# Differential attention in a token mixer: scores of each map from its own 32 channels instead of from masked copies of the keys

## The chip, the cores and the metric

The kernel runs on one core of a Trainium2 chip. The metric is the device time of one execution in microseconds; of several runs the median is given. Engines are named as in the profile: PE is TensorE's matmul, PEld its weight load, DVE VectorE, ACT ScalarE, POOL GpSimd, SP SyncE, which issues the DMAs.

## What is computed

Two networks run one after the other on a sequence of 256 tokens with 1024 features, batch 1, in float32. The first is one block (gated linear attentions, a recurrent unit, a convolved feed-forward part). The second has two layers of: feed-forward, token mixers, feed-forward, each with a layer norm. The token mixers are four attentions side by side (window, MLA, axial, differential) whose outputs are joined and multiplied by `w_out`. The change lies in the differential one, four heads, each with two maps of 32 channels (`DIFF_HEADS = 4`, `DIFF_QK = 32`, `DIFF_V = 64`):

```python
def _mixer_diff(d, lam_params, subln_g, slopes, layer_idx):
    q, k, v = jnp.split(d, [H * 2 * DIFF_QK, H * 4 * DIFF_QK], axis=-1)
    q = q.reshape(B, S, H, 2, DIFF_QK)
    k = k.reshape(B, S, H, 2, DIFF_QK)
    ...
        s = jnp.einsum('bqhmd,bkhmd->bhmqk', qi, k).astype(jnp.float32) * scale + bias[None, :, None]
        p = jax.nn.softmax(s, axis=-1)
        w = p[:, :, 0] - lam * p[:, :, 1]
        return jnp.einsum('bhqk,bkhd->bqhd', w.astype(v.dtype), v)
    ...
    o = _rms_norm(o, subln_g) * (1.0 - lam_init)
```

So each head has two score matrices, each over 32 channels of its own, two softmaxes, and the difference of the two.

## The kernel before

All 256 tokens stay on the chip, in two tiles of 128. Weights stream in from memory in pieces; each is split into a high and a low part (`piece`, line 92: ACT writes the high part, DVE or POOL the rest), and every product of activations and weights is three matmuls (`mm3`, lines 131 to 133; in the feed-forward parts lines 208 to 214 and 346). Attention scores and the products with the values are plain float32 matmuls.

`mixers2` (line 481) is the token mixer and runs once for each of the two layers. Its order is a plan written out by hand (line 732), which `weave` (line 449) plays: tokens such as `d2`, `u1` or `m0` are projections, `ax0`, `win0`, `mla0`, `diff0` queue the units of an attention for a token tile, and each `-` starts the next unit and takes each unit that is under way one stage further, the newest first. A unit is one head pair or, for `diff`, one head. After the plan comes the output projection (`contract`, line 745, its matmuls in lines 208, 211 and 214), in chunks that become ready as the attentions finish. This is the order of the program; within the data's dependencies a scheduler reorders each engine's instructions ahead of the launch, by a simulated timeline, and places the buffers and the semaphores.

The differential attention before the change:

- `diff_in` (line 639) is called as `d2` for the keys and as `d0` for the queries. The projection gives channels by tokens: 128 rows are 4 (head, map) pairs of 32 channels, two such groups `j`. For the keys, `d2` writes four copies of the projection into `dk` (line 637), copy `r` being multiplied by a column of 0 and 1 (`dmask`) that keeps the 32 channels of pair `r` alone. For the queries, `d0` writes one scaled copy, `dq`. `evac` (line 472) does each copy, alternately on ACT (line 475) and on DVE (lines 477, 479). `dk` shares its buffer (`tag="kzd"`) with `ct6`, a tile that the projection `u1` (`mla_up`) reads last.
- `diff(t)` (line 677) makes four units for token tile `t`. A unit for head `2 j + i` computes both maps with one matmul: all 128 rows of `dq`, times copies `2 i` and `2 i + 1` of `dk`, 512 columns (line 683). The zeros in the copies leave the right 32 channels.
- `softmax_head` (line 363) adds the bias and takes the maximum on DVE, one instruction for each map (line 379), then ACT takes the exponential (line 383). The unit goes on with the difference of the maps (lines 687 to 690), transposes on PE (line 149) and, in the last unit of a tile, the product with the values (line 704).
- The scores of all units, the outputs of the products with the values (lines 430, 434, 704) and some projections take their PSUM buffers from one pool, `mm`, of four, one bank each.

Other lines that are spoken of: 658 computes the scores of the window and axial attentions, from 64 rows (0 to 63 for unit 0, 64 to 127 for unit 1), two matmuls of 256 columns per unit into one buffer; 672 those of MLA, 96 rows; 928, in the first network, is a small matmul over 16 rows; 430 and 434 multiply by values with 64 columns of weights; 712 and 126 are DVE instructions that read the outputs of such products.

Of the kernel before, what the change touches and what calls it, by code (L numbers as in the profile page):

```python
# [11 lines left out]
F32 = mybir.dt.float32  # L12
F32R = mybir.dt.float32r
# [6 lines left out]
P = 128  # L20
T = 256
# [48 lines left out]
class Net:  # L70
# [292 lines left out]
    def softmax_head(self, ps, bias):  # L363


        nc, small = self.nc, self.small
        p = self.mix.tile([P, 2, T], F32, name="p_t", bufs=5)
        nm = small.tile([P, 2], F32, name="nm")
        sums = small.tile([P, 2], F32, name="sums")
        sink = None  # L370
        if bias is None:
            src = ps
            nc.vector.tensor_reduce(nm, ps, AX.X, ALU.max, negate=True)
        else:
            src = p
            mx = small.tile([P, 2], F32, name="mx")
            for j in range(2):
                tab, slope, sink = bias[j]
                nc.vector.tensor_tensor_reduce(p[:, j, :], ps[:, j, :], tab, -slope, -3e38 if sink is None else sink,
                                               ALU.add, ALU.max, mx[:, j : j + 1])  # L380
            nc.vector.tensor_scalar(nm, mx, -1.0, None, ALU.mult)
        for j in range(2):
            nc.scalar.activation(p[:, j, :], src[:, j, :], AF.Exp, bias=nm[:, j : j + 1], accum_out=sums[:, j : j + 1])
        es = None
        if sink is not None:
            es = small.tile([P, 2], F32, name="es")
            for j in range(2):
                nc.scalar.activation(es[:, j : j + 1], bias[j][2], AF.Exp, bias=nm[:, j : j + 1])
        return p, sums, es
# [91 lines left out]
    def mixers2(self, mix, l, post):  # L481
        nc, io = self.nc, self.io
        self.mix = mix
        pp, C = self.pp, self.C
        tsls = [slice(t * P, (t + 1) * P) for t in range(NT)]
# [5 lines left out]
        sink, gq, gk, lam4 = bp[:, 0:4], bp[:, 4:68], bp[:, 68:132], bp[:, 132:260]  # L491
# [33 lines left out]
            return groups[nm]  # L525

        kro = [mix.tile([P, 32], F32, name=f"kro{t}") for t in range(NT)]
        ct6 = mix.tile([P, 6, T], F32R, name="ct6", tag="kzd")
        cth, ctl = ct6[:, 0:3, :], ct6[:, 3:6, :]
        axv = mix.tile([P, NT, P], F32, name="axv")  # L530
        axq = mix.tile([P, 2, T], F32, name="axq")
# [102 lines left out]


        dq = mix.tile([P, 2, T], F32, name="dq")
        dk = mix.tile([P, 2, 4, T], F32, name="dk", tag="kzd")

        def diff_in(js):
            ks, n = group("diff")  # L640
            ps = self.proj_bank([P, 2, T])
            for j in js:
                self.proj_feat(ks, ps[:, j % 2, :], lambda w: w[:, j * P : (j + 1) * P])
                if j < 2:
                    self.evac(dq[:, j, :], ps[:, j, :], C["difq"][:, j : j + 1])
            if js[0] == 2:
                for r in range(4):
                    self.evac(dk[:, :, r, :], ps, C["dmask"][:, r : r + 1])


        slopes = [2.0 ** -(i + 1) for i in range(8)]
# [25 lines left out]
        def diff(t):  # L677
            hold = {}

            def run(j, i):  # L680
                h = 2 * j + i
                ps = self.mm.tile([P, 2, T], F32, name="mm_t")
                nc.tensor.matmul(ps, lhsT=dq[:, j, tsls[t]], rhs=dk[:, j, 2 * i : 2 * i + 2, :], start=True, stop=True)  # L683
                yield
                p, sums, _ = self.softmax_head(ps, [(C["dist"][:, t * T : (t + 1) * T], slopes[4 + h], None)] * 2)
                yield
# [585 lines left out]
    def setup(self):  # L1272
# [8 lines left out]
        for nm, w in CONSTS:  # L1281
# [5 lines left out]
        return ctile  # L1287


CONSTS = (("dist", 512), ("distw", 512), ("mlc", 64), ("mls", 64), ("axc", 128), ("axs", 128), ("winq", 2), ("difq", 2),  # L1290
          ("dmask", 4))
NCONST = sum(w for _, w in CONSTS)


def constants():

    f = np.float32
    pos = np.arange(T)
    dist = np.abs(pos[:, None] - pos[None, :]).astype(f)
    distw = np.where(dist <= 128, dist, f(1e32)).astype(f)  # L1300

    def angles(p, dim):
        inv = (f(10000.0) ** (-np.arange(0, dim, 2, dtype=f) / f(dim))).astype(f)
        a = p.astype(f)[:, None] * inv[None, :]
        return np.cos(a).astype(f), np.sin(a).astype(f)

    def tok(a):
        return a.reshape(NT, P, -1).transpose(1, 0, 2).reshape(P, -1)

    c, s = angles(pos, 32)  # L1310
    out = {"dist": tok(dist), "distw": tok(distw), "mlc": tok(np.concatenate([c, c], 1)),
           "mls": tok(np.concatenate([-s, s], 1))}
    cr, sr = angles(pos // 64, 32)
    cc, sc = angles(pos % 64, 32)
    out["axc"] = tok(np.concatenate([cr, cr, cc, cc], 1))
    out["axs"] = tok(np.concatenate([-sr, sr, -sc, sc], 1))
    p = np.arange(P)
    winq = np.zeros((P, 2))
    difq = np.zeros((P, 2))
    for j in range(2):  # L1320
        head = 2 * (p // 64) + j
        winq[:, j] = -0.125 * 2.0 ** (head + 1)
        head = 2 * j + p // 64
        difq[:, j] = -(32.0 ** -0.5) * 2.0 ** (head + 5)
    out["dmask"] = (p[:, None] // 32 == np.arange(4)).astype(f)
    out["winq"], out["difq"] = winq.astype(f), difq.astype(f)
    return np.ascontiguousarray(np.concatenate([out[nm] for nm, _ in CONSTS], 1).astype(f))

# [126 lines left out]
```

## Time and profile before

| | |
|---|---|
| median of 3 runs | 1340.91 us (1339.16 to 1342.98) |
| the profiled execution's own time | 1341.36 us |
| its span, first to last instruction | 1339.6 us |
| mean granted TensorE clock in the span | 0.994 |
| busy: PE, PEld | 1299.8 us (97%), 1092.4 us (82%) |
| busy: DVE, ACT, POOL | 887.1 us (66%), 730.3 us (55%), 558.8 us (42%) |
| chain of waits: PE, POOL, DVE, issue | 80%, 7%, 5%, 3% |

The span begins with the first instruction and ends with the last, so the execution's own time is somewhat longer. Matmuls are pipelined: the duration of a record reaches beyond the start of the next, and the distance between the starts tells what one costs. A granted clock of 1.00 is TensorE's full 2.4 GHz, 0.50 is 1.2 GHz. The token mixers lie between 525 and 645 us (first layer) and between 1022 and 1143 us (second layer). A float32 matmul shows as two records and an fp32r one as one.

### The profile page before, as it was taken

The numbers are of one execution on the slowest core, as the hardware profiler recorded it, in microseconds if no ns is written. First come the engines' busy times: TensorE is split into PE (matmuls) and PEld (weight loads), VectorE is DVE, ScalarE is ACT, GpSimd is POOL, SyncE is SP. The second block draws the span as 40 slices with busy tenths as digits, with TensorE's granted clock in tenths as the row PEclk, the third lists the DMA queues.
The fourth block names the chain that finished last, engine by engine and source line by source line (L and its number), as shares of the span: only waits on it lengthen the run. The fifth ranks groups of instructions, "written<-read, shape, count | busy, mean of one in ns | idle before, by whom it ended". The sixth has DMA issues, their size and how long they took to land.

```text
span 1339.6 us, 19335 instructions
## 1 busy us (share of the span) xinstructions
PE 1299.8 (97%) x7028; PEld 1092.4 (82%) x7028; DVE 887.1 (66%) x1402; ACT 730.3 (55%) x1282; POOL 558.8 (42%) x542
## 2 busy tenths in 40 slices
PE   7888899999999999999999999999999999999997
PEld 6767788888888888877888888888888877888886
DVE  5798588863667736677767645576726678766644
ACT  5775466654555543475556644465533666565540
POOL 5563433333533335830534434343436831434430
PEclk9999999999999999999999999999999999999999
DMA  6523545575655564550565564655664550655560
GB/s 220 189 64 118 188 157 186 186 217 166 216 172 187 186 213 147 181 168 7 187 211 185 185 220 146 217 189 189 209 191 138 165 159 1 219 190 188 188 205 32
DMA packets 63922, 227.19 MB, mean 170 GB/s; under 512 B 7105, under 2 KB 8145, under 8 KB 63058
## 3 DMA queue, kind: packets, MB, share of 16 engines
q1 hardware_dynamic: 63826, 225.95, 52.5%
q8 instruction: 55, 0.90, 0.3%
q14 instruction: 41, 0.34, 0.1%
HBM read 224.88 MB, written 1.05 MB: 169 GB/s over the span
## 4 chain that ended last, share of the span: by engine, by line
PE 80%; POOL 7%; DVE 5%; issue 3%; DMA 2%; ACT 2%; SPq 0%; DVEq 0%; ACTq 0%; POOLq 0%
PE mm_t L346 38%; PE acc_t L214 5%; PE acc_t L208 5%; PE acc_t L211 5%; PE mm_t L208 3%; PE mm_t L214 3%; PE mm_t L211 3%; POOL wl_t L111 3%; PE mm_t L133 3%; PE mm_t L131 3%; PE mm_t L132 3%; PE tp_t L149 2%; PE mm_t L430 1%; PE mm_t L683 1%; PE acc_t L131 1%
## 5 line engine op out<-in xcount | busy, mean ns | idle before, releaser
L111 POOL TENSOR_TENSOR wl_t<-raw,wh_t 128x512 fp32r<-128x512 f32 (+3 forms) x270 | 407.6, 1532 | 580.1 <-ACT wh_t L108 558.8
L111 DVE TENSOR_TENSOR wl_t<-raw,wh_t 128x1024 fp32r<-128x1024 f32 (+2 forms) x272 | 393.0, 1451 | 246.2 <-ACT wh_t L108 245.2
L108 ACT ACTIVATE wh_t<-raw 128x1024 fp32r<-128x1024 f32 (+2 forms) x407 | 416.5, 1039 | 232.3 <-PE mm_t L214 134.2
L346 PE MATMUL mm_t<-xx,wh_t 128*128 128x512 f32 x1456 | 501.6, 398 | 0.0
L346 PE MATMUL mm_t<-xx,wl_t 128*128 128x256 f32 x1456 | 379.4, 281 | 0.0
L346 PEld LDWEIGHTS mm_t<-xx,wh_t 128*128 128x128 f32 x1456 | 261.7, 188 | 49.3
L346 PEld LDWEIGHTS mm_t<-xx,wl_t 128*128 128x128 f32 x1456 | 274.9, 189 | 16.8
L349 DVE TENSOR_TENSOR sum<-sum,mm_t 128x256 f32<-128x256 f32 x182 | 74.4, 413 | 34.5 <-ACT sum L348 34.5
L348 ACT ACTIVATE sum<-mm_t 128x256 f32<-128x256 f32 x182 | 67.7, 372 | 39.0 <-PE mm_t L346 39.0
L208 PE MATMUL mm_t<-wh_t,hh 128*128 128x512 f32 x218 | 85.2, 391 | 0.0
L131 PE MATMUL mm_t<-wh_t,xx 128*128 128x512 f32 (+2 forms) x224 | 84.3, 376 | 0.8 <-ACT xx L125 0.8
L208 PE MATMUL acc_t<-wh_t,hh 128*128 128x512 f32 x218 | 84.9, 389 | 0.0
L211 PE MATMUL mm_t<-wl_t,hh 128*128 128x512 f32 x218 | 84.8, 389 | 0.0
L211 PE MATMUL acc_t<-wl_t,hh 128*128 128x512 f32 x218 | 84.8, 389 | 0.0
L132 PE MATMUL mm_t<-wl_t,xx 128*128 128x512 f32 (+2 forms) x224 | 83.5, 373 | 0.0
L133 PE MATMUL mm_t<-wh_t,xx 128*128 128x512 f32 (+2 forms) x224 | 82.6, 374 | 0.1
L214 PE MATMUL acc_t<-wh_t,hl 128*128 128x512 f32 x218 | 71.8, 389 | 0.0
L125 ACT ACTIVATE hh<-ht 128x256 fp32r<-128x256 f32 x72 | 30.1, 418 | 71.5 <-DVE ht L294 71.5
L214 PE MATMUL mm_t<-wh_t,hl 128*128 128x512 f32 x218 | 68.1, 389 | 0.0
L131 PE MATMUL acc_t<-xx,wh_t 128*128 128x256 f32 x176 | 52.3, 297 | 4.9 <-ACT wh_t L108 2.7
L126 DVE TENSOR_TENSOR hl<-ht,hh 128x256 fp32r<-128x256 f32 x72 | 37.8, 525 | 25.8 <-ACT hh L125 25.6
L292 ACT ACTIVATE sum<-sum 128x256 f32<-128x256 f32 x72 | 29.5, 409 | 41.7 <-DVE sum L349 41.7
(336 smaller groups left out, 2066.2 us busy)
## 6 DMA issues: line engine op xcount, KB each, us to landing
raw<-in_wgu_dram SPq DMA_DIRECT2D x176, 512.0 KB, 4.4
raw<-in_wd_dram SPq DMA_DIRECT2D x109, 512.0 KB, 4.4
raw<-in_gv_dram SPq DMA_DIRECT2D x42, 512.0 KB, 4.5
raw<-in_w_in_dram SPq DMA_DIRECT2D x36, 512.0 KB, 4.4
raw<-in_wo_dram SPq DMA_DIRECT2D x24, 512.0 KB, 3.7
gb<-in_ln_dram SPq DMA_DIRECT2D x6, 1024.0 KB, 4.7
raw<-in_w_in_dram SPq DMA_DIRECT2D x16, 384.0 KB, 3.5
raw<-in_w_in_dram SPq DMA_DIRECT2D x8, 416.0 KB, 3.5
```

What stands on the lines that cost most here:

```text
L108: nc.scalar.activation(hv, raw, AF.Copy)
L111: eng.tensor_tensor(lv[:, x : x + m], raw[:, x : x + m], hv.bitcast(F32)[:, x : x + m], ALU.subtract)
L126: self.nc.vector.tensor_tensor(dst_l, src, dst_h.bitcast(F32), ALU.subtract)
L131: mm(out, lhsT=lhs[0], rhs=rhs[0], start=start, stop=False, **kw)
L132: mm(out, lhsT=lhs[0], rhs=rhs[1], start=False, stop=False, **kw)
L133: mm(out, lhsT=lhs[1], rhs=rhs[0], start=False, stop=stop, **kw)
L208: m = self.nc.tensor.matmul(ps[t][h], lhsT=lh, rhs=wh[:, sl], start=first, stop=False)
L211: self.nc.tensor.matmul(ps[t][h], lhsT=lh, rhs=wl[:, sl], start=False, stop=False)
L214: self.nc.tensor.matmul(ps[t][h], lhsT=ll, rhs=wh[:, sl], start=False, stop=last)
L346: nc.tensor.matmul(out, lhsT=lhsT, rhs=rhs, start=k == 0 and i == 0, stop=k == NK - 1 and i == 1)
L348: nc.scalar.activation(r, ps[:, 1, :], AF.Copy)
L349: nc.vector.tensor_tensor(r, r, ps[:, 0, :], ALU.add)
```

## The change

The keys are kept once, as the projection gives them, without masks (`dk` has a quarter of its size), and `dk` and `ct6` get buffers of their own. A unit issues two matmuls, one for each map, over the 32 rows `64 i + 32 m` onwards of `dq` and `dk`, 256 columns each, into two buffers of the pool `mm`; `softmax_head` takes the list of the two. The constants lose the four columns of `dmask`.

```diff
@@ softmax_head
-                nc.vector.tensor_tensor_reduce(p[:, j, :], ps[:, j, :], tab, -slope, -3e38 if sink is None else sink,
+                nc.vector.tensor_tensor_reduce(p[:, j, :], ps[j] if isinstance(ps, list) else ps[:, j, :], tab, -slope, -3e38 if sink is None else sink,
                                                ALU.add, ALU.max, mx[:, j : j + 1])
@@ mixers2
-        ct6 = mix.tile([P, 6, T], F32R, name="ct6", tag="kzd")
+        ct6 = mix.tile([P, 6, T], F32R, name="ct6")
...
-        dk = mix.tile([P, 2, 4, T], F32, name="dk", tag="kzd")
+        dk = mix.tile([P, 2, T], F32, name="dk")
@@ diff_in
             if js[0] == 2:
-                for r in range(4):
-                    self.evac(dk[:, :, r, :], ps, C["dmask"][:, r : r + 1])
+                self.evac(dk, ps)
@@ diff, run
                 h = 2 * j + i
-                ps = self.mm.tile([P, 2, T], F32, name="mm_t")
-                nc.tensor.matmul(ps, lhsT=dq[:, j, tsls[t]], rhs=dk[:, j, 2 * i : 2 * i + 2, :], start=True, stop=True)
+
+                ps = [self.mm.tile([P, T], F32, name="mm_t") for _ in range(2)]
+                for m in range(2):
+                    a = slice(64 * i + 32 * m, 64 * i + 32 * m + 32)
+                    nc.tensor.matmul(ps[m], lhsT=dq[a, j, tsls[t]], rhs=dk[a, j, :], start=True, stop=True)
                 yield
@@ constants
-CONSTS = (("dist", 512), ("distw", 512), ("mlc", 64), ("mls", 64), ("axc", 128), ("axs", 128), ("winq", 2), ("difq", 2),
-          ("dmask", 4))
+CONSTS = (("dist", 512), ("distw", 512), ("mlc", 64), ("mls", 64), ("axc", 128), ("axs", 128), ("winq", 2), ("difq", 2))
...
-    out["dmask"] = (p[:, None] // 32 == np.arange(4)).astype(f)
```

## Rows read from the trace of the kernel before

**Rows 1.** View by windows: stretch, its us, busy us (instructions) of PE, PEld, DVE, ACT, POOL, PEclk, DMA.

```profile
595.00:645.00 50.00, 49.75 (x269) 34.97 (x268) 40.34 (x137) 30.50 (x88) 10.70 (x9) 1.00 0.17 54
645.00:860.00 215.00, 214.50 (x1096) 181.77 (x1095) 133.75 (x171) 111.75 (x168) 88.57 (x62) 1.00 0.61 198
...
1092.00:1143.00 51.00, 51.00 (x268) 35.10 (x267) 42.31 (x138) 30.45 (x87) 11.61 (x8) 1.00 0.17 53
```

**Rows 2.** Timeline of PE, around a diff unit: start us, us, engine, line, operation.

```profile
1108.69 1.02 PE L683 MATMUL mm_t<-dk,dq 128*128 128x512 f32 x2
1109.56 0.60 PE L149 MATMUL tp_t<-ident,p_t 128*128 128x128 f32 x4
```

**Rows 3.** Timeline of PE, around two MLA score units.

```profile
587.83 1.89 PE L672 MATMUL mm_t<-mqk 96*128 96x256 f32 x8
589.56 0.60 PE L149 MATMUL tp_t<-ident,p_t 128*128 128x128 f32 x4
```

**Rows 4.** Line 658: ns min/median/max, first and last start; 567.0 to 568.2, 573.4 to 574.6.

```profile
L658 PE MATMUL mm_t<-axk,axq x8: 376/376/480, 567.1 to 567.8; 64*128 64x256 f32 x8
...
L658 PE MATMUL mm_t<-wk,wq x4: 376/376/480, 573.5 to 574.3; 64*128 64x256 f32 x4
```

**Rows 5.** Timeline of PE, around the 16-row matmul of the first network.

```profile
46.99 0.69 PE L928 MATMUL mm_t<-glr,gup 16*128 16x256 f32 x2
47.62 0.39 PE L132 MATMUL acc_t<-xx,wh_t 128*128 128x256 f32 x1
```

**Rows 6.** Timeline of PE, around one 64-row unit among full-height matmuls.

```profile
573.00 0.60 PE L149 MATMUL tp_t<-ident,p_t 128*128 128x128 f32 x4
573.53 1.13 PE L658 MATMUL mm_t<-wk,wq 64*128 64x256 f32 x4
574.59 0.50 PE L131 MATMUL acc_t<-wh_t,ct 128*128 128x512 f32 x1
574.93 0.40 PE L132 MATMUL acc_t<-wl_t,ct 128*128 128x512 f32 x1
575.16 0.39 PE L133 MATMUL acc_t<-wh_t,ct 128*128 128x512 f32 x1
```

**Rows 7.** Timeline of PE, the first two diff units of the first layer.

```profile
594.56 1.08 PE L430 MATMUL mm_t<-pts,wdv 128*64 128x256 f32 x4
595.57 1.13 PE L683 MATMUL mm_t<-dk,dq 128*128 128x512 f32 x2
596.53 0.60 PE L149 MATMUL tp_t<-ident,p_t 128*128 128x128 f32 x4
596.97 1.02 PE L683 MATMUL mm_t<-dk,dq 128*128 128x512 f32 x2
```

**Rows 8.** Timeline, two diff units back to back; DVE's reads of two other buffers.

```profile
615.74 1.98 PE L683 MATMUL mm_t<-dk,dq 128*128 128x512 f32 x4
...
617.65 1.08 PE L430 MATMUL mm_t<-pts,axv 128*64 128x256 f32 x4
...
618.53 0.42 DVE L712 TENSOR_TENSOR do<-mm_t,ms 128x256 f32<-128x256 f32 x1
...
619.19 0.42 DVE L126 TENSOR_TENSOR ol<-mm_t,oh 128x256 fp32r<-128x256 f32 x1 [0.24 <-ACT oh L125]
```

**Rows 9.** Tile dk, its evacuations: ns min/median/max, first and last start.

```profile
L479 DVE TENSOR_SCALAR dk<-acc_t,ctile x4: 737/744/750, 584.2 to 1083.7; 128x512 f32<-128x512 f32 x4
L475 ACT ACTIVATE dk<-acc_t,ctile x4: 680/688/690, 585.8 to 1082.9; 128x512 f32<-128x512 f32 x4
```

**Rows 10.** Chain that ended last: first diff score and last projection matmuls, both layers.

```profile
595.63 1.06 PE mm_t L683 x2
...
641.12 0.66 PE acc_t L214 x2
...
1092.78 1.06 PE mm_t L683 x2
...
1139.47 0.66 PE acc_t L214 x2
```

## The prediction

> **What bounds the kernel now.** I read the stages first (the view by windows), then TensorE's instructions in order of time, then single lines and the chain of waits. The change touches only the token mixers of the second network, which run twice. The second half of each, where all the attention units run, is full of matmuls: PE is busy 49.75 of 50 us in one layer and 51.00 of 51 in the other, at a granted clock of 1.00 (the 2.4 GHz level), with DVE at about four fifths and ACT at three fifths; the stage behind has PE busy 214.5 of 215 us [rows 1]. A busy PE says little by itself, but the starts of the matmuls follow each other at their normal distance, because the scheduler fills every gap with matmuls of the output projection (lines 208 to 214). So in this half a microsecond of matmul time saved is a microsecond saved, as long as such fillers are ready, and a microsecond wasted is paid.
>
> **The score matmul now.** Each float32 matmul shows as two records. A diff unit (line 683) has two records of 512 columns over the full 128 rows: from its start to the next instruction 0.87 us, or 0.43 a record [rows 2]. There are 16 units: 2 layers, 2 token tiles, 4 heads. A record of 256 columns takes half of that: eight of line 672 last 1.73 us, 0.216 each [rows 3].
>
> **The score matmul afterwards: two maps, 32 rows each, 256 columns, two records each.** No row shows 32 channels in two maps at once; the nearest are the 64-row scores of line 658. There, eight records (two units, on rows 0 to 63 and 64 to 127, a buffer each) start between 567.1 and 567.8, while four records of one unit alone start between 573.5 and 574.3 [rows 4]: eight cost the time of four. So matmuls on different rows of the array run side by side, and a pair of maps should cost the time of one: 2 x 0.216 = 0.43 us instead of 0.86. The 16-row matmul of line 928 shows that a quarter-height one has the same pace: 0.63 us for two records [rows 5], as against 2 x 0.216 plus the 0.20 that comes next.
>
> That 0.20 is the price of changing the array's form. Around the lone four records: four transposes take 0.53 us up to the start where four take 0.44 elsewhere [rows 6, 7], so 0.09 to enter; the four records last 1.06, not 0.86, so 0.20 for a weight load that nothing covers and for leaving; and the first full-height matmul behind lasts 0.34 where the next lasts 0.23, so 0.11 [rows 6]. In all 0.40 us for a visit among full-height work. Half-width matmuls (lines 430, 434, 64 columns of weights) are a form of their own as well: a diff unit right behind one lasts 0.96, not 0.86 [rows 7], and four records between two of them last 1.91, not 1.72 [rows 8]. Some of the price is therefore paid already.
>
> The 16 units by what stands around them in the trace:
> - Five lie between full-height matmuls, as one does in [rows 2]. Now 0.86; then 0.09 + 0.20 + 0.43 + 0.01 (the second map's offset) + 0.11 = 0.84. Saved 0.02 each, 0.1 in all.
> - Four follow a half-width matmul and precede full-height work [rows 7]. Now 0.96; then 0.20 + 0.43 + 0.01 + 0.11 = 0.75. Saved 0.21 each, 0.84.
> - One lies between a half-width matmul and a 64-row one. Now 0.96 + 0.09; then 0.64. Saved 0.41.
> - Three times two units stand back to back behind a half-width matmul, as in [rows 8]: six units. If the two are parted by full-height work, the savings are 0.23 once and 0.43 twice, 1.1 in all. If they stay together but run one after the other, 2.3. If all four maps run abreast, 3.6.
>
> I take 1.1 for the last, because of the buffers. The score pool has four, and a unit now takes two of them. At 615.74 two others are still held: one is read by DVE at 618.53, one at 619.19 [rows 8]. The first unit then takes the remaining two, and the second must wait until DVE has read the first. Read in the same way, four of the 16 units start with fewer than two buffers free. Sum: 0.1 + 0.84 + 0.41 + 1.1 = 2.45, say **2.5 us less**; the bounds of the pair's cost are 5.0 less (3.6 for the last term) and, if the maps of a pair don't overlap at all, 16 x 0.43 = 6.9 more than the forecast, so 4.4 more than now.
>
> The Trainium skill (TensorE: Matmul & The Clock Gate, Part 3, "The mechanism") says that matmuls start and end strictly in program order. By that rule a pair would be three records deep, not two, since the second map's first pass stands behind the first map's second, and the sum would be 1341.9. The trace doesn't bear the rule out: in the program all four records of one unit of line 658 stand ahead of the other's, and yet they share the time [rows 4].
>
> **The other edits.** dk is one evacuation per layer instead of four of 0.69 to 0.74 us, two on each engine [rows 9]. That frees at least 2.1 us of ACT and DVE per layer, but the evacuations start at 584.2 to 585.8 in the first layer and the first score that reads dk starts at 595.57 [rows 7, 9]. I cost it at nothing: some 7 us of cover. Were the cover gone, three evacuations in series would be 2.1 us a layer, 4.2 in all. dk also leaves the buffer that it shared with ct6; the matmuls that read ct6 (u1) are issued on PE ahead of the projection that feeds dk, so this wait ends nothing. The constants lose 4 of 1416 columns, on one DMA far ahead of use; nothing else moves on SP or POOL. The softmax's two DVE reads go to two buffers; same instructions.
>
> Line 473 alternates the engines at every evacuation. With one where four were, all later evacuations up to the next dk change engine. The two layers run the same program with opposite alternation now and show what this and other chance of the schedule are worth: from the first diff score to the last projection matmuls of the chain 45.5 us in one, 46.7 in the other [rows 10], so up to 1.2 us a layer, either way. I take zero and put 2.4 into the range.
>
> The profiled execution took 1341.36 us, its span 1339.6; it stands 0.45 above the median of 1340.91. Against its own time the sum gives 1338.9, against the median **1338.4**.
>
> **Rivals.** A measurement of this kernel can tell about 0.3%, 4.0 us, from no change.
> - *More than the forecast.* The back-to-back units go abreast, or the schedule gains by the freed ACT and DVE time. For it: the eight records in the time of four [rows 4], and DVE at four fifths. Against it: the held buffers. 5.0 less, 1335.9, and with the chance of the schedule down to 1333.5.
> - *In program order.* The second map starts only behind the first map's second record: 16 x 0.216 = 3.5 us back, 1341.9. Against it [rows 4]. The Trainium skill's rule above is this mechanism. If nothing overlaps at all (32-row parts are not in the trace), 1345.3.
> - *The buffers part the pairs: slower.* In place of the removed copies comes a wait of the second map for its own buffer. It stands in PE's queue, and everything on PE is behind it; or the scheduler puts a filler between the maps. Then each map is a visit of its own: 2 x 0.84 instead of 0.84, 0.84 lost per unit. The place is where units follow each other closely while two outputs are held. Three parted units eat the 2.5 us; from eight of 16 (2.5 + 4.0 = 6.5 = 8 x 0.84) the kernel is measurably slower, 1342.6 with five parted, 1345.1 with eight, 1351.8 with all. For it: four units surely lack a second buffer. Against it: the other twelve don't. The Trainium skill (TensorEngine Tiling (Array Packing), "Gotcha 1: PSUM Pressure") warns of this: parts in different rows write to different banks, which raises the demand for banks.
> - *Hidden.* The fillers run out, or the softmax on DVE sets the pace of the units: 1340.9.
>
> **How the numbers follow.** Forecast 0.46, and with its scatter of 2.4 us either way 0.12 of that is beyond 0.3% and 0.34 within. More than the forecast 0.20, all faster. In program order 0.08 (0.07 within, 0.01 slower); no overlap 0.05 (0.04 slower, 0.01 within). Parted pairs 0.15 (0.12 slower, 0.03 within). Hidden 0.06, within. Faster 0.12 + 0.20 = 0.32, within 0.34 + 0.07 + 0.01 + 0.03 + 0.06 = 0.51, slower 0.01 + 0.04 + 0.12 = 0.17. The range goes from 1333.5 (5.0 and the scatter) to 1344.0 (between six parted units, 1343.5, and seven); beyond lie the upper half of the parted pairs and most of no overlap.
>
> **What would show it.** Right: line 683 has 64 records of 256 columns on 32 rows; in a pair the four start within some 0.35 us (two at once, two 0.32 us later), and from the pair's start to the next full-height matmul it is 0.64, not 0.86. The two stages each get shorter by about 1.2 us, and all others stay. Wrong: the records of a pair start one behind another 0.2 us apart (program order, or no overlap); or another line's matmul stands between the two maps, or a wait of line 683 for DVE's line 379 appears among PE's waits (buffers); or the pairs cost 0.64 and the stage is as long as before (hidden). A change in any stage outside the two mixers that is over 1 us would mean that the schedule moved for another reason.

## The result and the profile after

The change made the kernel slower. The median is 1348.95 us (18 runs, 1343.97 to 1359.73) beside 1342.11 us for the kernel before (18 runs, 1339.16 to 1344.03): ratio 1.006, 95% interval 1.0049 to 1.0072. The prediction was 1338.4, with 1333.5 to 1344.0 as its range.

The 18 runs fall into two groups. Nine took 1343.97 to 1347.13 us at a mean granted clock of 0.991 to 0.994, nine 1350.77 to 1359.73 us at 0.983 to 0.988. The first group's median is 1346.47, 4.4 us above before; a later comparison, all of whose runs of the change were of this kind, gave 1.0029 (1.0018 to 1.0041). The profiled execution took 1343.97 us at 0.994, so its trace shows the first part of the loss alone. Two executions of later comparisons, 2137.28 us of the kernel before and 4518.68 us of `held`, lie far outside everything else; nothing below rests on them.

The page of the changed kernel, engines' busy time in the span, and the view by windows (stretch, its us, busy us and instructions of PE, PEld, DVE, ACT, POOL, then PEclk and DMA); lines of the second network stand 1 or 2 away from those of before:

```profile
PE 1300.0 (97%) x7060; PEld 1092.1 (81%) x7060; DVE 885.1 (66%) x1399; ACT 730.7 (54%) x1279; POOL 559.1 (42%) x542
```

```profile
593.00:643.00 50.00, 50.00 (x275) 34.85 (x274) 40.24 (x135) 29.38 (x86) 9.50 (x8) 1.00 0.16 53
643.00:858.00 215.00, 214.50 (x1096) 181.76 (x1095) 134.91 (x173) 112.17 (x167) 89.19 (x62) 1.00 0.61 196
1091.00:1142.00 51.00, 47.59 (x259) 32.19 (x258) 39.95 (x136) 28.84 (x84) 6.71 (x6) 1.00 0.15 46
...
1091.00:1107.00 16.00, 16.00 (x82) 9.38 (x80) 11.70 (x38) 7.66 (x21) 3.51 (x2) 1.00 0.41 131
1107.00:1123.00 16.00, 12.59 (x76) 8.07 (x73) 13.73 (x62) 11.29 (x40) 1.03 (x1) 1.00 0.01 2
```

Against [rows 1]: the stage behind is the same, the first layer's half is as full as before, and the second layer's half has lost 3.4 us of PE's time, all of it between 1107 and 1123 us. There DVE is the busiest engine (13.73 of 16 us), and PE waits five times. The view of waits of that half, PE alone (it had none before):

```profile
PE acc_t L208 <- ACT oh L125: 1.0, 1, 1.0
PE mm_t L706 <- ACT p_t L383: 0.9, 1, 0.9
PE tp_t L149 <- ACT pts L424: 0.7, 1, 0.7
PE mm_t L657 <- DVE mx L379: 0.5, 1, 0.5
PE tp_t L149 <- DVE do L714: 0.3, 1, 0.3
```

The pair itself does what was forecast. The timeline of PE, start us, us, engine, line, operation: first a whole pair (four records, line 685), then the next unit, parted (two records, and the other two 2.88 us later), then the stretch with the waits.

```profile
1091.23 0.70 PE L685 MATMUL mm_t<-dk,dq 32*128 32x256 f32 x4
1091.86 0.66 PE L149 MATMUL tp_t<-ident,p_t 128*128 128x128 f32 x4
...
1094.81 0.69 PE L685 MATMUL mm_t<-dk,dq 32*128 32x256 f32 x2
1095.43 0.50 PE L214 MATMUL acc_t<-wh_t,ol 128*128 128x512 f32 x1
...
1097.69 0.69 PE L685 MATMUL mm_t<-dk,dq 32*128 32x256 f32 x2
1098.31 0.66 PE L434 MATMUL mm_t<-pts,mlv 128*64 128x128 f32 x8
...
1107.80 0.44 PE L149 MATMUL tp_t<-ident,p_t 128*128 128x128 f32 x2
1109.09 1.07 PE L706 MATMUL mm_t<-wdv,pts 128*128 128x64 f32 x8 [0.86 <-ACT p_t L383]
...
1120.96 0.60 PE L149 MATMUL tp_t<-ident,p_t 128*128 128x128 f32 x4
1122.59 0.50 PE L208 MATMUL acc_t<-wh_t,oh 128*128 128x512 f32 x1 [1.03 <-ACT oh L125]
```

Four records of a pair take 0.63 us up to the next start, two of a single map 0.62. So a parted unit pays its whole visit (a run of its matmuls between others) twice. Six of the 16 units are parted, three a layer; the 16 units make 22 visits. The line's own view shows the first step of the softmax, DVE's line 379, waiting for these matmuls 8 times, 7.1 us in all (before 4 times, 2.9 us):

```profile
L685 PE MATMUL mm_t<-dk,dq x64: 374/426/479, 593.3 to 1116.9; 32*128 32x256 f32 x64
...
  DVE p_t L379: 7.1, 8
```

**Where the time went.** I cut both traces at the same matmuls: each mixer from the last matmul of line 214 of the feed-forward before it to the first of line 346 behind it. The rest of the kernel from the first line 346 on takes, without the two mixers, 878.3 to 878.4 us in every profile of the change and 878.3 before. What comes ahead of that differs between executions of one kernel (163.0 to 166.6 us in six profiles of the change, 166.6 in the one of before). The two mixers take 145.36 and 149.34 us before, 294.7 in all; after, 147.20 and 152.59, 299.8. So all of it is in the mixers: +5.1 us, of which the execution gave 2.5 back ahead of them.

From the first diff score to the next stage I took the distance of each matmul's start to the next, less the distance that it has in an unbroken row of its kind. What is over is either a switch of the array's form (60 to 140 ns each) or a gap (more). One kind of step looks like a gap and is none: where a diff unit of the kernel before is followed by a projection matmul, that one's start is recorded 0.03 us behind the start of the unit's second record, and its own step is then 0.63 us and not 0.23. The 0.40 over belongs to the diff score. Timeline of PE before:

```profile
596.97 1.02 PE L683 MATMUL mm_t<-dk,dq 128*128 128x512 f32 x2
597.42 0.79 PE L208 MATMUL acc_t<-wh_t,oh 128*128 128x512 f32 x1
598.06 0.40 PE L211 MATMUL acc_t<-wl_t,oh 128*128 128x512 f32 x1
```

There are three such steps in the first layer and two in the second; they are counted under matmuls here.

| us, after minus before | matmuls | switches (number) | gaps | other | sum |
|---|---|---|---|---|---|
| first layer (75.98 to 77.59) | -1.3 | +3.2 (33 to 64) | -0.2 | +0.0 | +1.6 |
| second layer (77.19 to 81.27) | -2.4 | +2.2 (43 to 65) | +4.0 | +0.3 | +4.1 |

So the overlap did save matmul time, 3.8 us in the two layers. 53 more switches cost 5.3, and gaps in the second layer 4.0. The added switches stand at the diff scores: before, 18 of the 76 were at line 683 or next to it, now 71 of the 129 are at line 685 or next to it.

### The profile page after: what moved, and what is told of

Its sections match the earlier page's. It is cut to its first block, busy times and chain, and to the rows that moved or that the text cites. A ratio compares the mean times of both kernels' runs of the same rounds, so it can differ in the third digit from the quotient of the medians.

```text
span 1342.2 us, 19383 instructions
## 1 busy us (share of the span) xinstructions
PE 1300.0 (97%) x7060; PEld 1092.1 (81%) x7060; DVE 885.1 (66%) x1399; ACT 730.7 (54%) x1279; POOL 559.1 (42%) x542
## 4 chain that ended last, share of the span: by engine, by line
PE 83%; DVE 5%; POOL 5%; issue 3%; DMA 2%; ACT 2%; SPq 0%; DVEq 0%; ACTq 0%; POOLq 0%
PE mm_t L346 38%; PE acc_t L214 5%; PE acc_t L208 5%; PE acc_t L211 5%; PE mm_t L214 3%; PE mm_t L208 3%; PE mm_t L211 3%; PE mm_t L131 3%; PE mm_t L133 3%; PE mm_t L132 3%; PE tp_t L149 3%; POOL wl_t L111 2%; PE acc_t L131 1%; PE acc_t L132 1%; PE acc_t L133 1%
```

## The experiments

All runs in one table, in the order of the text. "Mixers" is the sum of the two as above, from the profile (294.7 before). The time of before is that of the same comparison. For `held` it is the median of three executions, 1348.58 to 1357.86 us.

| run | us | before | ratio, 95% | mixers |
|---|---|---|---|---|
| again (the change) | 1345.53 | 1341.79 | 1.0018 to 1.0041 | 300.4 |
| two_banks | 1345.92 | 1341.79 | 1.0015 to 1.0041 | 300.9 |
| form64 | 1341.32 | 1341.79 | 0.9986 to 1.0005 | 295.2 |
| flip | 1347.71 | 1341.79 | 1.0032 to 1.0090 | 299.5 |
| stacked | 1344.47 | 1341.76 | 1.0011 to 1.0054 | 308.2 |
| stacked2 | 1344.89 | 1341.76 | 1.0017 to 1.0044 | 297.7 |
| mm3 | 1345.99 | 1341.76 | 1.0019 to 1.0043 | 296.4 |
| mm5 | 1370.93 | 1341.76 | 1.0186 to 1.0235 | 295.7 |
| mla_first | 1348.57 | 1340.94 | 1.0045 to 1.0079 | 301.4 |
| mla_first_old | 1342.57 | 1340.94 | 1.0001 to 1.0022 | 297.6 |
| mla_first_st2 | 1342.86 | 1340.94 | 1.0006 to 1.0024 | 296.5 |
| held | 1354.46 | 1340.47 | 1.0089 to 1.0142 | 300.5 |

**The change again.** No edit.

> The changed kernel, unchanged, for its scatter: its 18 executions went from 1343.97 to 1359.73 us with a mean granted clock from 0.994 down to 0.983, while the only profile so far is of its fastest one. All theories: executions between 1343.9 and 1360 us, the long ones at the lower clocks. The idle theory (PE runs out of ready work in the second layer's mixer, 4.5 us of gaps there in the profile, and the clock then falls) expects the half-level stretches that are new in a profile at a low clock between 1100 and 1180 us. The form theory (work on 32 of 128 rows makes the clock fall) expects them in both mixers, behind the diff scores, also around 590 to 645 us. If they lie elsewhere, both fall.

Seven executions, 1344.59 to 1346.64 us at 0.992 and 0.993. The stages from the first diff score on were 77.59 and 81.23 us, the same as in the first profile to 0.04: this loss belongs to the program, not to an execution. No long execution was among them.

**Buffers without the form, and the form without buffers.** Two kernels from the one before, masked copies kept:

```diff
 two_banks
...
-                ps = self.mm.tile([P, 2, T], F32, name="mm_t")
-                nc.tensor.matmul(ps, lhsT=dq[:, j, tsls[t]], rhs=dk[:, j, 2 * i : 2 * i + 2, :], start=True, stop=True)
+                ps = [self.mm.tile([P, T], F32, name="mm_t") for _ in range(2)]
+                for m in range(2):
+                    nc.tensor.matmul(ps[m], lhsT=dq[:, j, tsls[t]], rhs=dk[:, j, 2 * i + m, :], start=True, stop=True)
 form64
...
-                nc.tensor.matmul(ps, lhsT=dq[:, j, tsls[t]], rhs=dk[:, j, 2 * i : 2 * i + 2, :], start=True, stop=True)
+                a = slice(64 * i, 64 * i + 64)
+                nc.tensor.matmul(ps, lhsT=dq[a, j, tsls[t]], rhs=dk[a, j, 2 * i : 2 * i + 2, :], start=True, stop=True)
```

> The kernel before, with its masked copies and full-height scores, but the two maps of a unit written by two matmuls of 256 columns into two buffers of the score pool. Only the buffers change, the array's form does not. Buffer theory with parted pairs priced by the form (0.84 us per parted unit is the price of a second visit in another form): parting full-height maps costs nothing, so 0 to +1.2 us against before, and no dips of the clock (0.993 to 0.994). Buffer theory with waiting (the second buffer itself stalls PE and starves the softmax): +2 us and more, PE waits for DVE in the second layer's mixer and executions at 0.983 to 0.992. Form theory: as before within 1.2 us, clock 0.994.

> The kernel before with its masked copies and one buffer per unit, but the score matmul reads only the 64 rows of its head (512 columns as before). Only the array's form changes, the buffers do not. By the prices of the prediction (0.40 us a visit among full-height work, 0.21 behind a half-width matmul, two neighbouring units on different halves side by side): 5 x 0.40 + 4 x 0.21 - 3 x 0.65 = +0.9 us against before. Form theory of the clock (part of the array idle makes it fall): executions at 0.983 to 0.992, some 5 us longer. Idle theory: clock 0.993 to 0.994.

The two-buffer kernel loses 4.1 us by the medians, as much as the change (3.7), although its diff scores stay at full height; the 64-row form alone loses nothing (-0.5 us). The view by windows of `two_banks`, then of `form64`, the same two halves as above:

```profile
596.00:646.00 50.00, 50.00 (x281) 37.87 (x280) 40.49 (x137) 30.26 (x88) 9.83 (x8) 1.00 0.16 53
1094.00:1145.00 51.00, 48.51 (x260) 35.52 (x259) 39.97 (x136) 29.29 (x84) 8.24 (x7) 1.00 0.16 52
```

```profile
597.00:647.00 50.00, 49.75 (x271) 34.73 (x269) 39.97 (x137) 30.52 (x89) 10.57 (x9) 1.00 0.17 55
1094.00:1145.00 51.00, 51.00 (x270) 34.98 (x269) 42.25 (x138) 31.00 (x88) 11.90 (x9) 1.00 0.16 54
```

With two buffers a unit PE runs dry in the second layer (48.51 of 51 us), without them it doesn't. Its gaps there are 4.5 us, as in the change (4.6; 0.6 before). So the waiting version of the buffer theory holds for the time: a unit that needs two of four buffers starts late. The clock that it went with, 0.983 to 0.992, did not come: the five executions had 0.992 to 0.994. The fourth unit of the second layer has its second map 13.1 us behind the first score of that layer in `two_banks` and 13.9 in the change; before, the unit starts at 10.2, and in `form64` at 10.8. Four units are parted in `two_banks`, at no price of form, and still it loses as much as the change with six. The price of the 64-row form, forecast as +0.9, came out as +0.5 in the mixers: 22 more switches, paid by neighbours side by side.

**The evacuations' alternation.** The change plus one toggle behind dk:

```diff
                 self.evac(dk, ps)
+                self.flip ^= 1
```

> The changed kernel with one more toggle of the evacuation's alternation behind dk, so that all later evacuations use the engines that they used in the kernel before (dk itself stays one evacuation). In program order four of the 16 units are parted, not six. Theory of parted pairs: 2 x 0.84 = 1.7 us shorter than the changed kernel at the same clock, so about 1342.3 us; if the gaps of the second layer's mixer shrink with it, the clock's dips go too and the median comes down from 1349 to 1343. Form theory: the visits are the same in number or nearly so, dips stay, median 1347 to 1349. Chance of the schedule: anything from 1340 to 1346 at clock 0.994, with no relation to the number of parted units.

> The changed kernel with the alternation of before, whose executions were long in five of ten cases (1349 to 1364 us at clocks of 0.990 to 0.978), for a profile of a long one. Clock theory: a long execution has half-level time in one of the two mixers, 2 us of it for each us of excess, where PE works through narrow matmuls with gaps between; a short one (1344 to 1346 us) has none there. If a long one has its half-level time outside the mixers, the theory falls.

> As the run before it, for the same question and with the same numbers.

Four units are parted, not six, and the mixers take 299.1 to 299.6 us in three profiles; from the first diff score on the two layers take 0.7 us less than in the change. The alternation is worth less than the 1.2 us a layer that I allowed, and alternation and two parted units fewer together are worth 0.7 here, not 1.7: this run does not bear out 0.84 for each parted unit. The timed runs went up to 1363.81 us at 0.978. The three profiles, at 1344.62, 1344.74 and 1343.24 us, are short ones. Their only half-level time in the mixers is 3.4 us at 1032.8 to 1035.1 us, ahead of the first diff score, which the kernel before has as well (at 1033.5).

**One buffer fewer, one more.** The kernel before with three score buffers, and the change with five (and one buffer for transposes):

```diff
 mm3
-        self.mm = pool("mm", 4, space=PSUM)
+        self.mm = pool("mm", 3, space=PSUM)
 mm5
-        self.mm = pool("mm", 4, space=PSUM)
+        self.mm = pool("mm", 5, space=PSUM)
...
-        self.tp = pool("tp", 2, space=PSUM)
+        self.tp = pool("tp", 1, space=PSUM)
```

> The kernel before with three score buffers in place of four, nothing else. Buffer theory: the same signature as the change without any of its edits: units later, projection matmuls used up early, gaps of PE of 0.4 us and more in the second layer's mixer, the two stages from the first diff score to the next stage 3 to 6 us longer in all (76.0 and 77.2 us before, 77.6 and 81.3 in the change). Rival (only the parting of a unit's two maps costs): no map is parted here, so within 1 us of before.

> The changed kernel with five score buffers, the fifth taken from the transposes (one left of two). Buffer theory: fewer parted units, the fourth unit of the second layer earlier than 12.9 us behind the first, gaps of that mixer smaller than the 4.6 us of the change, and the stage from the first diff score on back from 81.3 towards 78; against it works the single transpose buffer, which can bring waits of its own (transposes behind ACT's copy of the tile before). Form theory: the visits stay 0.63 us each and the stage stays above 80.

Three buffers cost the mixers 1.7 us, not 3 to 6, and all of it in the first layer (+2.1, the second -0.4); the rest of that kernel's loss lies outside them (7.1 us more ahead of the first line 346, 4.2 less behind it). The expected signature did not show: three units in flight are nearly enough, two are not. The change with five buffers is much slower as a whole: behind the first line 346 everything but the mixers takes 905 us, not 878, which I put down to the single transpose buffer. But its mixers take 295.7 us, 1.0 above before and 4.1 below the change, with 9 visits a layer instead of 11 and the second map of the second layer's fourth unit at 9.6 us, not 13.9. Fewer parted units, as expected, it does not have: three a layer are parted still, but some of the halves run beside another unit's pair. From the first diff score on, its two stages take 75.76 and 76.52 us, less than before (75.98 and 77.19), although in each of them TensorE ran for 3.4 us at the 1.2 GHz level, which in the kernel before it never does there. View by windows of these stretches, then the timeline of PE into the second one, which begins behind a wait for ACT:

```profile
627.80:631.20 3.40, 3.23 (x11) 1.75 (x14) 2.27 (x9) 1.70 (x6) 1.28 (x1) 0.50 0.00 0
1136.40:1139.80 3.40, 3.39 (x11) 1.91 (x14) 2.11 (x8) 1.53 (x5) 1.29 (x1) 0.50 0.02 5
```

```profile
1134.81 0.61 PE L149 MATMUL tp_t<-ident,p_t 128*128 128x128 f32 x4
1136.41 1.11 PE L149 MATMUL tp_t<-ident,p_t 128*128 128x128 f32 x4 [0.99 <-ACT pts L424]
```

That is the buffer theory's clearest support: a buffer more takes most of the loss away. The kernel before with five buffers and one for transposes was not run, so what the transposes cost in these stages is not known apart.

**One buffer per unit on 32 rows.** Columns of the projection laid out so that the two maps of a head share 32 rows (tile `m` holds map `m` of all heads), one buffer, the two matmuls one behind the other (`stacked`); then the four matmuls of two heads issued together (`stacked2`, not shown; nor are the edits to the order of the columns and to the queries' scales):

```diff
 stacked
...
-                ps = [self.mm.tile([P, T], F32, name="mm_t") for _ in range(2)]
+                ps = self.mm.tile([P, 2, T], F32, name="mm_t")
+                a = slice(32 * h, 32 * h + 32)
                 for m in range(2):
-                    a = slice(64 * i + 32 * m, 64 * i + 32 * m + 32)
-                    nc.tensor.matmul(ps[m], lhsT=dq[a, j, tsls[t]], rhs=dk[a, j, :], start=True, stop=True)
+                    nc.tensor.matmul(ps[:, m, :], lhsT=dq[a, m, tsls[t]], rhs=dk[a, m, :], start=True, stop=True)
...
```

> The change without its second buffer: the columns of the projection are laid out so that both maps of a head sit on the same 32 rows in two tiles, so each map still reads its own 32 channels and there are no masked copies, but the two matmuls of a unit write one buffer, one behind the other. Buffer theory (two of four buffers per unit delay the units, the 24 ready projection matmuls are used up early, and PE then waits): as the kernel before within 1.5 us, like the 64-row form (1341.3); no gaps of a microsecond in the second layer's mixer; the fourth unit of that layer starts some 10 us behind the first, as before (10.2), not 12.9. Form theory (32 of 128 rows is what costs): +3.5 us, as the changed kernel on this chip (1345.5).

> As the run before, and the scores of two heads are issued together, four matmuls on two sets of 32 rows into two buffers, so that the heads run side by side as the maps of the change do. Two units then cost one visit of some 0.86 + 0.40 = 1.26 us and not 1.72 to 1.82: 8 x 0.5 = 4 us less than before, if PE never waits. Buffer theory: two buffers serve two units here, half of what the change takes, so most of it should show: 1338 to 1341. If taking two buffers at one moment is what delays (not their number per unit), the gaps of the second layer come back: 1342 to 1346.

Both fell short. `stacked2` lies where taking two buffers at one moment was to put it (1342 to 1346). `stacked` is 2.7 us slower than before where I expected no difference: in the first layer it has 55 switches for 33 (+2.2 us) and less overlap of the other scores. Its units are not late: the fourth of the second layer starts at 8.6 us. The 32-row form thus costs something by itself, where `form64` happened to pay nothing; buffers are not the only cause. `stacked2` has the smallest matmul time (1.3 and 2.0 us less than before) and gives it back in switches (+1.6 and +1.0) and gaps (+1.7 and +2.8).

The profile of `stacked` is the one that caught a long execution (1352.99 us, clock 0.986). The view by windows of its second layer:

```profile
1094.00:1112.00 18.00, 18.00 (x98) 11.76 (x98) 13.92 (x54) 9.75 (x31) 3.26 (x2) 1.00 0.36 117
1112.00:1134.00 22.00, 22.00 (x67) 14.84 (x66) 13.30 (x60) 10.45 (x38) 1.04 (x1) 0.53 0.00 1
1134.00:1145.00 11.00, 10.08 (x69) 8.01 (x68) 3.98 (x11) 3.44 (x9) 1.01 (x1) 1.00 0.00 0
```

and its timeline, four matmuls of one shape before the fall and in it, and eight diff records in it (eight took 1.06 us at 1102.31):

```profile
1094.94 1.08 PE L430 MATMUL mm_t<-pts,wdv 128*64 128x256 f32 x4
...
1116.20 1.97 PE L430 MATMUL mm_t<-pts,axv 128*64 128x256 f32 x4
1118.10 2.08 PE L685 MATMUL mm_t<-dk,dq 32*128 32x256 f32 x8
```

For some 20.5 us PE ran at the 1.2 GHz level; the stage took 87.8 us. PE had been busy all the 18 us ahead at 1.00, with scores of 32 and 64 rows and outputs of 64 columns in turn. This is where about 10 us of a long execution went in that kernel (half of 20.5, as its matmuls took about twice their time: 1.97 us for 1.08).

**Fillers.** By the timeline, 24 projection matmuls (the axial and the window chunk of the first token tile) have been started 12.0 us behind the second layer's first diff score in the change, 15.5 before; the next come at 31.4 and 27.6. In the first layer it is 15.0 and 15.1, then 28.0 and 25.9. In the next run the latent-attention chunk comes ahead of the differential one, for the first token tile, so 36 are ready:

```diff
...
             rows = [(k, kk, w) for c, w in held for kk, k in enumerate(ks[c])]
+            if self.order == [2, 0, 3, 1]:
+                if t == 0:
+                    rows = rows[:4] + rows[6:] + rows[4:6]
+                self.k_order = [row[0] for row in rows]
```

> The changed kernel; in the output projection of the first token tile the rows of the latent-attention unit are taken before those of the differential unit, so that 12 more projection matmuls are ready while the last diff unit of that tile is on its way (36 and not 24). Starvation theory (the change makes the diff units late, the 24 ready fillers are used up 12 us behind the first diff score, and PE then has nothing): the 4.6 us of gaps in the second layer shrink to about 1.5, that stage goes from 81.3 to some 78 us, and the first layer's by less than 1; in all about 3 us less than the changed kernel, 1342.5 where that takes 1345.5. If gaps are only a symptom (the softmax chain sets the end of the stage): the stage stays at 81, 1345.5.

> The same order of rows in the kernel before, as the control and as a candidate that could beat both. Starvation theory: its gaps in the two stages are 2.3 and 1.5 us, the greater part single steps of 0.4 us that no filler ends, so at most 1 us is to be had: 1340.5 to 1342, and the gain of the changed kernel from the same edit is larger by 2 us. Otherwise both gain the same.

> The same order of rows with the shared buffer per head and two heads issued together (keys once, 32 rows, no more buffers than before). Its two stages were 78.0 and 79.1 us with gaps of 2.8 and 3.4, and its matmuls' own time is 1.2 us a layer less than before (66.8 against 66.9 and 68.0). Starvation theory: gaps shrink to 1.5 each, the stages come to 76.7 and 77.2, some 3 us less than without the order, 1341.5 to 1342; a kernel faster than before is only in reach if the visits' switches (4.8 and 5.4 us, 3.2 and 4.3 before) shrink as well.

A miss as a remedy. In the change the second layer's gaps fell from 4.6 to 2.2 us, but its stage only from 81.3 to 80.1: units that had been side by side came apart again (matmul time +1.4). In the first layer, which had no such gaps, the stage grew from 77.6 to 80.8, since the fillers now went ahead of the units. The kernel before loses 1.6 us with the same edit, `stacked2` gains 1.2 in its mixers and stays above before. The order of the fillers also moved the units: eight are parted here, not six. So the gaps are real, but filling them does not bring the units forward.

**Pairs kept together.** Each buffer first takes one column at full height, and both maps follow both of these:

```diff
+                got = [nc.tensor.matmul(b[:, 0:1], lhsT=dq[:, j, tsls[t]], rhs=dk[:, j, 0:1], start=True, stop=True) for b in ps]
                 for m in range(2):
                     a = slice(64 * i + 32 * m, 64 * i + 32 * m + 32)
-                    nc.tensor.matmul(ps[m], lhsT=dq[a, j, tsls[t]], rhs=dk[a, j, :], start=True, stop=True)
+                    mt = nc.tensor.matmul(ps[m], lhsT=dq[a, j, tsls[t]], rhs=dk[a, j, :], start=True, stop=True)
+                    for g in got:
+                        self.follow(mt, g)
```

> The changed kernel with its pairs kept together: each of the two buffers first takes a one-column matmul over the full height (overwritten afterwards), and both maps come only behind both of these, so that no other matmul stands between the maps. Theory of the parted pairs (a parted unit costs a second visit of 0.84 us): the six parted units cost nothing more, the switches of 60 to 140 ns fall from 64 and 65 to some 50 a layer, and the two stages without the added matmuls (64 records, counted by themselves, at most 0.11 us each by the 128-column transposes, so up to 7 us) come near before's, 76 and 77 us. Late-unit theory (two buffers per unit leave two units in flight, not four, and the fourth unit of a layer starts late whatever stands between its maps): the pairs are whole, yet the fourth unit of the second layer still starts later than 12 us behind the first, and without the added matmuls the two stages stay 4 us and more above before's.

All 16 pairs are whole. Timeline of PE, one unit of the second layer with its one-column matmuls apart, then the longest wait, then PE's waits in that half:

```profile
1108.08 0.38 PE L683 MATMUL mm_t<-dk,dq 128*128 128x1 f32 x2
...
1109.26 0.28 PE L683 MATMUL mm_t<-dk,dq 128*128 128x1 f32 x2
1109.47 0.70 PE L686 MATMUL mm_t<-dk,dq 32*128 32x256 f32 x4
...
1118.30 1.11 PE L709 MATMUL mm_t<-wdv,pts 128*128 128x64 f32 x8 [1.56 <-DVE pts L477]
```

```profile
PE mm_t L709 <- DVE pts L477: 1.6, 1, 1.6
PE mm_t L709 <- ACT p_t L383: 1.0, 1, 1.0
PE tp_t L149 <- DVE p_t L420: 0.7, 1, 0.7
```

The added matmuls take 3.2 us of each stage by their starts and the next. Without them the stages would be 78.05 - 3.2 = 74.9 and 81.04 - 3.3 = 77.8 us: 1.1 less and 0.6 more than before, and 2.7 and 3.5 less than in the change. For three parted units a layer that is 0.9 and 1.2 us each (0.84 forecast), and the switches fall to 55 and 48 (some 50 forecast). The subtraction takes the added time as wholly on the path; in the first layer, where PE has no gaps but 0.8 us, that is nearly so, in the second (gaps 4.4 us) it credits too much. The units stay late there: the fourth starts its pair only at 13.4 us. So both theories hold a part. Parting costs about its price by this subtraction (`flip` gave less), and lateness brings the gaps of the second layer, which stay when the pairs are whole; but the two stages are not 4 us and more above before, as the late-unit theory asked.

**More profiles of the change**, for a long execution. No edit.

> The changed kernel once more for one profile. In one profile of the shared-buffer kernel the clock fell to its lower level for 20.5 us in the second layer's mixer, behind its run of narrow matmuls; all theories that put the long executions of the change down to the clock expect, if this execution is a long one (over 1349 us), half-level time of that kind in one of the two mixers, 10 us of it for every 5 us of excess. A short one (1344 to 1347 us) has no such stretch.

> The changed kernel for one profile. If this execution is a long one (over 1349 us) the excess is half-level time of the clock in one of the two mixers, 2 us of it for each us of excess, as in the shared-buffer kernel's profile; a short one (1342 to 1347 us) has none there, and its two stages are 77.6 and 81.3 us again to within 0.1 us.

> As the run before it: one more profile of the changed kernel, for the same question and with the same numbers.

> The changed kernel, for the same question: a long execution (over 1349 us) with half-level time in one of the two mixers, or a short one without.

All four were short: 1342.72, 1346.62, 1345.60 and 1345.85 us, stages of 77.57 to 77.59 and 81.23 to 81.27, and no half-level time in them; ahead of the first diff score three of the four have the 3.4 us at 1032 to 1036 us that the kernel before has. Where it lies in a long execution of the change itself stays open; only `stacked` shows one.

## Why the prediction was wrong

**The pair was right.** Forecast 0.64 us from a pair to the next full-height matmul, measured 0.63; the four records run two abreast. The rule that matmuls start and end strictly in program order (the Trainium skill, TensorE: Matmul & The Clock Gate, Part 3, "The mechanism") would have made a pair a third record longer than a single map, 0.62 + 0.216 = 0.84, if one map's two records stand ahead of the other's in PE's queue, which the profile does not show; the trace has 0.63, so by that reading it is not borne out here. With whole pairs (`held`, its added matmuls taken off) the first layer comes out 1.1 us below before, where I had forecast about 1.2 a layer; the second comes out 0.6 above.

**The step that failed** is the count of the buffers: "four of the 16 units start with fewer than two buffers free". I read it, and then let it count only for the units that stand back to back; the sum has no term for a unit that is parted. Six were (22 visits, not 16), and by the prediction's own price 6 x 0.84 = 5.0 us turn 2.5 less into 2.5 more, 1343.5. Even the four that I had found would have turned the sign (4 x 0.84 = 3.4). The price stood in the text, in the rival *Buffers part the pairs*, which got a chance of 0.15. That rival is what happened, in its mechanism (the sign set for it, another line's matmul between the two maps, stands in the trace at 1095.43); in size it falls short of even the shorter executions (median 1346.47), because the units' lateness, below, is in none of its terms. The Trainium skill (TensorEngine Tiling (Array Packing), "Gotcha 1: PSUM Pressure") names this demand for banks; `mm5` agrees: one more buffer takes 4.1 of the mixers' 5.1 us away.

**What also failed** is the classification by neighbours. It kept the order of before, in which five units stand among full-height work and four behind a half-width matmul. The scheduler orders PE anew when buffers come free at other times, and switches rose from 76 to 129 in the two stages, where I had counted one visit for each unit in its old place. The rise is at the diff scores.

**The condition "as long as such fillers are ready"** was not looked at. In the kernel before, too, no projection matmul starts between 15.1 and 25.9 us behind the first diff score in the first layer, and none between 15.5 and 27.6 in the second: there the units alone keep PE full, and nothing stands ready when they are late. In the second layer of the change the 24 ready ones have started by 12.0 us, the units are late, and PE waits 3.4 us (busy 47.59 of 51 us, before all of it). Only the rival *Hidden* spoke of fillers that run out, and it priced that at no change (1340.9, with a chance of 0.06); I took them as endless because the halves were full.

Put together, from the table: matmul time -3.8, switches +5.3, gaps +3.8, other +0.4, in all +5.7 us in the two stages. Six parted units at 0.84 would be 5.0 of it; they cost both switches and matmul time. Since the two causes act on each other (`two_banks` loses as much, without a narrow diff matmul), how much is parting and how much lateness is not shown. Any edit reorders PE anew as well, and kernels that have one buffer a unit moved by -0.4 to +2.4 us in a layer (`mm3`, `form64`, `mla_first_old`), so single microseconds in this account are not to be trusted.

**What held**: dk's fewer evacuations and ct6's own buffer are together worth nothing that can be told (up to the first diff score the mixers take 69.61 and 71.32 us, before 69.38 and 72.15; 69.4 to 69.8 and 71.0 to 72.1 in six profiles of the change); the alternation, with what it does to the pairs, is worth 0.7 us. All stages outside the mixers and behind the first line 346 together are the same to 0.2 us.

**What was not thought of** is the clock: half of the first comparison's executions lost another 4 to 13 us at a lower mean clock. I read the granted clock of one execution and took it as given. Over 1349 us were 9 of 29 executions of the change, 5 of 12 of `flip`, 2 of 10 of `stacked` and 1 of 10 of `stacked2`, and none of `two_banks`, `form64` or `mm3`. The cause is not settled, so of the 6.8 us between the two medians only the part that the short executions show, 4.4, is accounted for.

**No version beat both.** `form64` is level with before (0.9986 to 1.0005); everything with fewer masks or more overlap lost.

## What to carry to other kernels

Before a result is split over more buffers, divide the pool by what a unit takes: four buffers at two a unit are two units in flight, and here that was too few, while three buffers at one a unit cost the mixers 1.7 us and five at two a unit 1.0. A matmul that is made cheaper by running beside its twin is only cheaper while the two are issued together; when a buffer parts them, each pays the whole visit. And a stretch of PE that looks full has only as many fillers as are ready: count them (24 here), and find when the last is used and when the next are due.

## What the runs showed of the hardware that was not expected

Two maps on different 32 rows cost what one does, 0.63 against 0.62 us, and eight records of two heads on two sets of rows took 1.06 us (`stacked`, 1102.31 to 1103.37), as four records did in [rows 6]. A one-column float32 matmul at full height costs about 0.1 us a record (0.21 us for two, 1109.26 to 1109.47), like a transpose of 128 columns (0.44 us for four, [rows 7]). TensorE's clock fell to its 1.2 GHz level for 20.5 us in a stretch of `stacked` ahead of which PE had been busy for 18 us without a gap in the profile; in `mm5` it fell for 3.4 us in each mixer, once the matmuls resumed behind a wait of 1 us. Mean clocks (0.986 against 0.989 to 0.995 in `stacked`) say that not every execution of a program has such a long fall.
